# A decoder layer on one core: attention's steps draw products forward by a table, more rooms, other first loads, a later second norm

## The chip, the cores and the metric

The kernel runs on one core of a Trainium2 chip. The core has a matrix engine (PE, with its weight loads shown as PEld), a vector engine (DVE), a scalar engine (ACT), a general engine (POOL) and an engine that here issues transfers (SP). Each takes its instructions in order; they wait for one another through semaphores. The metric is the time of one execution on the device, in microseconds.

## The reference

One layer on x of 1024 tokens by 1024 features, all in float32:

```
h = rms_norm(x); proj = h @ w_in              # 256 pool columns, then q, k, v of 12 heads of 64
q, k = rope(q), rope(k)
pool_out = means over 2/4/8/16 tokens minus the token, per group @ w_pool, * pool_scale
attn_out = merge, by softmax denominators, of three windows: (128,1), (512,4), (2048,16)
x = x + rms_norm(concat(pool_out, attn_out) @ w_out)
h = rms_norm(x); f = (silu(h @ w_gate) * (h @ w_up)) @ w_down     # w_gate, w_up: 1024 x 2816
x = x + rms_norm(f)
```

## The kernel before

Products are float32 made of three passes: each operand is split into a high part (ACT, a rounding copy) and a low part (a subtraction on DVE or POOL), and high·high, high·low and low·high are summed in one bank. A pass is a matmul of 128 x 128 by 128, 256 or 512 columns. Features lie on partitions, tokens along the free dimension, in two halves of 512 (`h`).

The program has these stages.

1. **First loads.** x comes in eight tiles (`load_x`, L242 and L243 scale and split it), the first two weight tiles in two chunks (`load_w`, L155 and L159), and `first` makes q and k of head pair 0. The squares of x (L249, L251) feed the first norm.
2. **Attention.** Twelve *units*, each one pair of heads and one half. A unit runs `scores` (eight steps; DVE takes masked scores from a bank `ps_s` with a row minimum into `sx`, L556; ACT makes the exponentials in `pp`, L559), `merge` (small tiles `ex`, `em`, `dd`, `wv`; the two windows' sums are put together by two products `ps_s<-ex,ls`, L575 to L595), `weigh` (POOL, L611, or DVE, L609, multiply `pp` by `wv`) and `values`: `turn` transposes four blocks of `pp` into a bank `ps_t` (L119), ACT and DVE split it into `ptr` (L655, L656), and `product` multiplies `ptr` with v into `ps_o`; at the end of a head the low half is added (L691) and split into `mix` (L621, L623), which goes to memory (`mixd`, L628). v takes the way over memory: projected, split, written (`vd<-vs`, L475), read again in two orders (`v<-vd`, L504).
3. Beside it runs **fill**: the projections of the next pairs (ps_pj, and ropes of their results: `rsw`, `rco`, L323 to L328, DVE and POOL), v's projection and the pool mixer. They are lists of single products (`Fill`).
4. **Output projection** of both halves, then per half a `chain`: norm, sum with x, split for the next stage, squares of the new x (L1004, L1005) and its norm's factor (`s3.mean`, `s3.rows`).
5. **Gate, up and down**, in seven block products per block of columns (Strassen's scheme), and the last norm and sum.

What sets the order: a plan. Each list of steps has a start and an end in units (`PRM`), and `emit` sorts all steps by their time. PE's instructions stay in that written order; the others are placed by a scheduler that works from estimated times. Inside a step `await_` keeps a small model clock: where a result that the step needs is not due yet, it first draws fill products (`pull`), at most twelve:

```
    def await_(*keys):
        at = max([due.get(k, 0.0) for k in keys] or [0.0])
        n = 0
        while clock[0] < at and n < G["fl"]:
            ...
            pull()
            n += 1
```

Rooms: `pp` (also the tiles of x and other small loads) has 7 of 4 KB a partition, `ptr` 2, the raw weight tile `wraw` 2.

Of the kernel before, what the change touches and what calls it, by code (L numbers as in the profile page):

```python
# [15 lines left out]
P = 128  # L16
# [6 lines left out]
PPB = 7  # L23
PTB = 2
# [10 lines left out]
        'sqa': (1, 0, 0, 1, 0, 0, 0, 1),  # L35
        'we': (1, 1, 1, 0, 0, 0, 0, 0, 0, 0, 1, 1),
        'nt0': 0.505,
        'nt1': 0.51,
        'oq': (0, 1, 1, 1, 0, 0, 0, 1),
        'lag': 3.0,  # L40
        'fl': 12,
        'lt': 3.0,
        'ls': 2.2,
        'lm': 2.8,
        'lw': (3.5, 0.5),
        'nm': 0.02,
# [49 lines left out]
        'c0': (0.13, 0.2, 0.21, 0.6, 0.3, 0.7, 0.9, 0.99),
        'c1': (0.08, 0.17, 0.18, 0.8, 0.4, 0.95, 1.57, 1.7),
        'c2': ((0.95, 1.35), (1.4, 1.6)),
        'e0': ((0.26, 0), (0.42, 0), (0.47, 0.9)),
        'e1': (((1.08, 0), (1.28, 0), (1.3, 1.9)), ((2.0, 0), (2.01, 0), (2.02, 2.03)))}  # L100
# [10 lines left out]
def hybrid_block(ctx: ExitStack, tc: tile.TileContext, xT, w_in, w_v, w_pin, w_pool, w_out, w_gate, w_up, w_down,  # L111
# [6 lines left out]
    def turned_to(dst, src, by):  # L118
        return tc.keep_in_program_order(nc.tensor.transpose(dst, src, by))  # L119

# [33 lines left out]
    def split(dst, src, eng):  # L154
# [3 lines left out]
        for at in range(0, n, w):  # L158
            eng.tensor_tensor(dst[:, 1, at:at + w], src[:, at:at + w], dst[:, 0, at:at + w].bitcast(F32), ALU.subtract)  # L159
# [39 lines left out]
    nc.sync.dma_start(g1s, g1)  # L199
# [17 lines left out]
    w0r = [wpool.tile([P, 1024], F32, name="wraw", tag="wraw", bufs=2) for i in range(2)]  # L217
# [4 lines left out]

    def first(i, k):
        for a, b in PASSES:
            for h in range(2):
                mm(acc0[i, h], w0[i][:, a, k * P:(k + 1) * P], xk[k][:, b, h * 512:(h + 1) * 512],
                   start=(k == 0 and a + b == 0), stop=(k == NK - 1 and a == 1))

    def load_w(i, lo, hi):
# [3 lines left out]
        split(w0[i][:, :, sl], w0r[i][:, sl], nc.vector)  # L233

    xr0 = []

    def load_x(k, lo=0, hi=T):
        if lo == 0:
            xr0.append(att.tile([P, T], F32, name="xraw", tag="pp", bufs=PPB))
        r, sl = xr0[k], slice(lo, hi)  # L240
        nc.sync.dma_start(r[:, sl], xT[:, k, sl])
        nc.scalar.activation(xk[k][:, 0, sl], r[:, sl], AF.Copy, scale=g1s[:, k:k + 1])  # L242
        nc.vector.scalar_tensor_tensor(xk[k][:, 1, sl], r[:, sl], g1s[:, k:k + 1], xk[k][:, 0, sl].bitcast(F32),  # L243
                                       op0=ALU.mult, op1=ALU.subtract)

    def square(k):
        r = xr0[k]
        d = att.tile([P, T], F32, name="jk", tag="ptr", bufs=PTB) if k else sq
        nc.scalar.activation(d, r, AF.Square)  # L249
# [7 lines left out]
    for i in range(2):  # L257
        first(i, 0)
# [1308 lines left out]
```

## Time and profile before

| | us |
|---|---|
| median of 3 runs | 1169.71 |
| lowest and highest | 1167.99, 1169.85 |
| the profiled execution | 1170.79 |
| its span, first to last instruction | 1169.0 |

Busy time in that span: PE 1135.2 us (97%), weight loads 982.6 (84%), DVE 791.9 (68%), POOL 603.2 (52%), ACT 543.5 (46%). The mean granted clock of PE is 0.988 of its full speed. The span has three parts: first loads and attention up to some 465 us, the turn to the feed-forward part to some 512 us, and the feed-forward products to the end.

To read it: a row of a group gives line, engine, operation, what is written and read, and times in us; in rows of the order of time the bracket gives the idle time before an instruction and who ended it. A busy PE is one with some matmul in flight, not one at its peak. The line numbers are those of the kernel before.

### The profile page before, as it was taken

How to read it: one execution, taken by the hardware profiler on the slowest of the kernel's cores; microseconds unless marked ns; L12 is line 12 of the kernel's file. 1: busy time of each engine (PE TensorE's matmuls, PEld its weight loads, DVE VectorE, ACT ScalarE, POOL GpSimd, SP SyncE). 2: the span in 40 equal slices, each digit the busy share in tenths (PEclk: the TensorE clock that was granted, in tenths of full speed). 3: DMA queues.
4: the chain of work that ended last, by engine and by line, in shares of the span. 5: the costliest groups of instructions: out<-in, count | busy, mean ns of one | idle time of the engine just before them, and what ended most of it. 6: DMA issues, size and time to landing. Idle time of an engine off the chain costs nothing.

```text
span 1169.0 us, 17248 instructions
## 1 busy us (share of the span) xinstructions
PE 1135.2 (97%) x6134; PEld 982.6 (84%) x6134; DVE 791.9 (68%) x1477; ACT 543.5 (46%) x1033; POOL 603.2 (52%) x541
## 2 busy tenths in 40 slices
PE   8999999999998999999999999999999999999996
PEld 6998889989888888778888888888888888888896
DVE  7766778787887675869685665756565475454685
ACT  7356667665566674655432233223232335343430
POOL 0111546565565413150476667777665978656521
PEclk9999999999999999989999999999999999999998
DMA  7315151515124744732143544544535859766542
GB/s 270 102 60 181 37 181 37 168 49 181 55 73 146 286 163 163 272 106 90 52 174 135 198 162 175 186 173 161 206 128 188 281 198 378 240 204 191 183 144 72
DMA packets 85365, 188.51 MB, mean 161 GB/s; under 512 B 8736, under 2 KB 24352, under 8 KB 83872
## 3 DMA queue, kind: packets, MB, share of 16 engines
q1 hardware_dynamic: 84704, 186.90, 45.9%
q8 instruction: 48, 0.79, 0.3%
q10 hardware_dynamic: 576, 0.52, 0.1%
q14 instruction: 37, 0.30, 0.1%
HBM read 134.44 MB, written 52.95 MB: 160 GB/s over the span
## 4 chain that ended last, share of the span: by engine, by line
PE 83%; DVE 6%; ACT 4%; DMA 3%; issue 2%; POOL 1%; SPq 0%; ACTq 0%; POOLq 0%; DVEq 0%
PE ps_pj L116 28%; PE ps_o L116 22%; PE ps_s L116 21%; PE ps_t L116 9%; PE ps_t L119 2%; ACT pp L559 1%; DMA b<-in_w_out_dram 1%; DMA m<-mixd 1%; DMA mixd<-mix 1%; DVE k L348 1%; DMA xraw<-in_xT_dram 1%; DMA rw<-in_w_up_dram 0%; DVE ptr L656 0%; DVE whl L159 0%; DMA vd<-vs 0%
## 5 line engine op out<-in xcount | busy, mean ns | idle before, releaser
L116 PE MATMUL ps_pj<-x,whl 128*128 128x512 f32 x480 | 145.6, 417 | 0.0
L1221 POOL TENSOR_TENSOR fw<-rw,fw 128x512 fp32r<-128x512 f32 x74 | 101.6, 1399 | 61.3 <-ACT fw L1219 58.7
L611 POOL TENSOR_SCALAR pp<-pp,wv 128x256 f32<-128x256 f32 (+1 forms) x156 | 72.1, 482 | 103.8 <-DVE wv L595 51.0
L116 PE MATMUL ps_o<-tT,fw 128*128 128x512 f32 x504 | 117.5, 389 | 0.0
L159 POOL TENSOR_TENSOR whl<-wraw,whl 128x512 fp32r<-128x512 f32 x50 | 66.4, 1348 | 91.4 <-ACT whl L155 55.8
L116 PEld LDWEIGHTS ps_o<-tT,fw 128*128 128x128 f32 x504 | 94.6, 188 | 19.6
L559 ACT ACTIVATE pp<-pp,sx 128x128 f32<-128x128 f32 (+1 forms) x192 | 89.3, 468 | 30.1 <-DVE sx L556 29.6
L116 PEld LDWEIGHTS ps_pj<-x,whl 128*128 128x128 f32 x480 | 87.4, 194 | 10.2 <-POOL whl L159 0.4
L1221 POOL TENSOR_TENSOR whl<-rw,whl 128x512 fp32r<-128x512 f32 x42 | 61.1, 1479 | 58.3 <-ACT whl L1219 58.3
L1219 ACT ACTIVATE fw<-rw 128x1024 fp32r<-128x1024 f32 x37 | 38.5, 1057 | 97.5 <-DVE rw L1187 41.9
L116 PE MATMUL ps_pj<-whl,x 128*128 128x256 f32 x528 | 79.5, 291 | 0.0
L1363 POOL TENSOR_TENSOR op<-rw,op 128x512 fp32r<-128x512 f32 x38 | 59.9, 1577 | 37.3 <-ACT op L1362 36.0
L656 DVE TENSOR_TENSOR ptr<-ps_t,ptr 128x512 fp32r<-128x512 f32 (+1 forms) x84 | 56.2, 669 | 24.4 <-ACT ptr L655 23.8
L1362 ACT ACTIVATE op<-rw 128x1024 fp32r<-128x1024 f32 x38 | 40.2, 1060 | 66.9 <-PE ps_t L116 31.3
L325 POOL TENSOR_TENSOR rsw<-rsw,sinr 128x512 f32<-128x512 f32 x20 | 26.2, 1312 | 85.0 <-DVE rsw L323 85.0
L116 PEld LDWEIGHTS ps_pj<-whl,x 128*128 128x128 f32 x528 | 69.7, 194 | 0.4 <-DVE whl L159 0.2
L655 ACT ACTIVATE ptr<-ps_t 128x512 fp32r<-128x512 f32 (+1 forms) x84 | 48.4, 576 | 41.0 <-PE ps_t L119 39.7
L116 PE MATMUL ps_o<-ptr,v 128*128 128x128 f32 (+1 forms) x472 | 59.2, 259 | 5.4 <-DVE ptr L656 5.4
L116 PE MATMUL ps_pj<-b,fw 128*128 128x512 f32 x264 | 61.6, 389 | 0.0
L116 PEld LDWEIGHTS ps_o<-ptr,v 128*128 128x128 f32 x472 | 52.8, 165 | 9.8 <-DVE ptr L656 6.5
L116 PEld LDWEIGHTS ps_pj<-b,fw 128*128 128x128 f32 x264 | 49.5, 188 | 10.3
L116 PE MATMUL ps_s<-k,qh 128*128 128x128 f32 (+1 forms) x192 | 53.6, 291 | 0.3 <-DVE sx L556 0.2
(302 smaller groups left out, 2918.0 us busy)
## 6 DMA issues: line engine op xcount, KB each, us to landing
rw<-bd SPq DMA_DIRECT2D x77, 256.0 KB, 4.9
v<-vd SPq DMA_DIRECT2D x22, 512.0 KB, 4.4
rw<-wsd SPq DMA_DIRECT2D x44, 256.0 KB, 4.0
rw<-in_w_gate_dram SPq DMA_DIRECT2D x20, 512.0 KB, 3.6
rw<-in_w_up_dram SPq DMA_DIRECT2D x20, 512.0 KB, 4.6
bd<-p SPq DMA_DIRECT2D x33, 256.0 KB, 3.0
rw<-in_w_down_dram SPq DMA_DIRECT2D x33, 256.0 KB, 4.8
fw<-in_w_down_dram SPq DMA_DIRECT2D x16, 512.0 KB, 4.1
```

The costliest lines, as they stand in the source:

```text
L116: return tc.keep_in_program_order(nc.tensor.matmul(*a, **k))
L119: return tc.keep_in_program_order(nc.tensor.transpose(dst, src, by))
L159: eng.tensor_tensor(dst[:, 1, at:at + w], src[:, at:at + w], dst[:, 0, at:at + w].bitcast(F32), ALU.subtract)
L325: eng[0].tensor_tensor(s, s, sinr[:, sl], ALU.mult)
L559: nc.scalar.activation(pt[:, j, lo:], pt[:, j, lo:], AF.Exp, bias=sx[:, 0, side, j, hd, 0:1], scale=-1.0, accum_out=sx[:, 0, side, j, hd, ...
L611: nc.gpsimd.tensor_scalar(pv, pv, un.wv[:, side, j, hd:hd + 1], 1.0, op0=ALU.mult, op1=ALU.mult)
L655: nc.scalar.activation(ptr[:, 0, :w], t[:, :w], AF.Copy)
L656: nc.vector.tensor_tensor(ptr[:, 1, :w], t[:, :w], ptr[:, 0, :w].bitcast(F32), ALU.subtract)
L1219: nc.scalar.activation(w[n][:, :, 0], raw[n], AF.Copy)
L1221: low[0] = nc.gpsimd.tensor_tensor(w[n][:, i, 1], raw[n][:, i], w[n][:, i, 0].bitcast(F32), ALU.subtract)
L1362: nc.scalar.activation(w[:, :, 0], raw, AF.Copy)
L1363: nc.gpsimd.tensor_tensor(w[:, 0, 1], raw[:, 0], w[:, 0, 0].bitcast(F32), ALU.subtract)
```

## The change

It has five parts.

- The program's scratch memory for transfer descriptors is set to 1 KB, and three rooms are added: `pp` 8, `ptr` 3, `wraw` 3.
- A table `x` gives, by unit and step, a number of fill products that the step draws beside those of the model clock; a negative number lets the step begin earlier on that clock. Each unit has its own start and end times (`own`).
- The first loads come in another order, g1 on ACT's queue, x1 in two halves, the weights in chunks of two, two and four blocks; the first half tile of x gets its high part on DVE; the passes of x0 and x1 go by half.
- Half 0's second norm: its `mean` and `rows`, and the scaling of z by g3, leave the list of the output projection (`cut`) and stand 0.25, 0.42 and 0.25 to 0.7 into the list of the first gate and up products. Their results are held in their banks until the rows are there (`kept`). The weights of the second column block are loaded by steps of that list.
- More of DVE's instructions keep the written order (`pinned`), the pool mixer's products go by four tiles, and several times of the plan differ.

Three places, engine by engine. First DVE at the merge of unit 7 (pair 3, half 1), where `ex` is each window's sums, `rsw` and `rco` the rope of a projection and `ps_o`, `low` the end of a head. Before:

```order
L575 TENSOR_TENSOR ex<-sx,qdB 128x64
L691 TENSOR_TENSOR ps_o<-ps_o,low 64x512
L656 TENSOR_TENSOR ptr<-ps_t,ptr 128x512
L323 STREAM_SHUFFLE rsw<-ps_pj 128x512
L324 TENSOR_TENSOR rco<-ps_pj,cosr 128x512
L575 TENSOR_TENSOR ex<-sx,qdA 128x64
```

and after:

```order
L776 TENSOR_TENSOR ptr<-ps_t,ptr 128x512
L811 TENSOR_TENSOR ps_o<-ps_o,low 64x512
L694 TENSOR_TENSOR ex<-sx,qdA 128x64
L448 STREAM_SHUFFLE rsw<-ps_pj 128x512
L449 TENSOR_TENSOR rco<-ps_pj,cosr 128x512
```

The rope now stands behind the second `ex`. In unit 1 the rope stays before it and the addition into `ps_o` moves behind; in unit 5 both stand before it:

```order
L448 STREAM_SHUFFLE rsw<-ps_pj 128x512
L449 TENSOR_TENSOR rco<-ps_pj,cosr 128x512
L811 TENSOR_TENSOR ps_o<-ps_o,low 64x512
L694 TENSOR_TENSOR ex<-sx,qdA 128x64
```

Second, PE at the end of the output projection of half 1 (`fw` is the mix, `b` the normed x of half 0, `ps_t` the first gate bank, `ones,sq` the sums of squares, `idt,nrr` a norm's rows). Before:

```order
L116 MATMUL ps_pj<-fw,whl 128x512 x24
L116 MATMUL ps_s<-fw,whl 128x512 x5
L116 MATMUL ps_o<-ones,sq 128x1 x4
L116 MATMUL ps_s<-fw,whl 128x512 x18
L119 MATMUL ps_o<-idt,nrr 128x128 x4
L116 MATMUL ps_s<-fw,whl 128x512
```

and after, where the same place has neither, and the first sums to come, 12 gate products later, are those of half 1's first norm:

```order
L193 MATMUL ps_pj<-fw,whl 128x512 x24
L193 MATMUL ps_s<-fw,whl 128x512 x24
L193 MATMUL ps_t<-b_5468,whl 128x512
L193 MATMUL ps_t<-b_5469,whl 128x512
L193 MATMUL ps_t<-b_5468,whl 128x512 x2
```

Third, SP's first transfers. Before:

```order
L199 DMA g1s<-in_g_dram 128x8
L241 DMA xraw<-in_xT_dram 128x512
L232 DMA wraw<-in_w_in_dram 128x256
L241 DMA xraw<-in_xT_dram 128x512
L232 DMA wraw<-in_w_in_dram 128x256
L241 DMA xraw<-in_xT_dram 128x1024
L232 DMA wraw<-in_w_in_dram 128x768 x2
L241 DMA xraw<-in_xT_dram 128x1024 x6
```

and after:

```order
L324 DMA wraw<-in_w_in_dram 128x256
L338 DMA xraw<-in_xT_dram 128x512
L324 DMA wraw<-in_w_in_dram 128x256
L338 DMA xraw<-in_xT_dram 128x512 x3
L324 DMA wraw<-in_w_in_dram 128x256 x2
L338 DMA xraw<-in_xT_dram 128x1024
L324 DMA wraw<-in_w_in_dram 128x512 x2
L338 DMA xraw<-in_xT_dram 128x1024 x5
```

x2 now stands behind 256 KB of weights where 768 KB stood, and x1 before them in two pieces.

The core of the diff:

```diff
-PPB = 7
-PTB = 2
+PPB = 8
+PTB = 3
...
+ 'own': {0: {'s0': 0.4799, 's1': 0.5663, 'm': 0.8618, 'w0': 1.0668, 'w1': 0.9699, 't0': 1.1072, 'v0': 1.259, 'v1': 1.9554},
...
+PRM["x"] = {(0, 'm'): 5, (0, 's', 0): 8, (0, 's', 1): 6, (0, 's', 2): 5, (0, 's', 3): 3, (0, 's', 4): 2, (0, 's', 6): 3,
...
-        r = own or wpool.tile([P, 1024], F32, name="wraw", tag="wraw", bufs=2)
+        r = own or wpool.tile([P, 1024], F32, name="wraw", tag="wraw", bufs=3)
...
-    nc.sync.dma_start(g1s, g1)
+    nc.scalar.dma_start(g1s, g1)
...
+    def split_x(k, lo=0, hi=T, fast=False):
+        r, sl = xr0[k], slice(lo, hi)
+        if fast:
+            pinned(nc.vector.tensor_scalar(xk[k][:, 0, sl], r[:, sl], g1s[:, k:k + 1], None, op0=ALU.mult))
+        else:
+            pinned(nc.scalar.activation(xk[k][:, 0, sl], r[:, sl], AF.Copy, scale=g1s[:, k:k + 1]))
...
+    fetch_w(0, 2, 0)
+    fetch_x(0, 0, 512)
+    fetch_w(0, 2, 1)
+    fetch_x(0, 512, T)
+    for h in range(2):
+        fetch_x(1, h * 512, h * 512 + 512)
     for i in range(2):
+        fetch_w(2, 4, i)
+    fetch_x(2)
     for i in range(2):
+        fetch_w(4, NK, i)
+    for k in range(3, PPB):
+        fetch_x(k)
...
+    for k in range(2):
+        for h in range(2):
+            for i, n in ((0, 0), (1, 0), (0, 2), (1, 2), (0, 1), (1, 1)):
+                part(i, h, k, n)
...
-    def await_(*keys):
+    def await_(*keys, step=None):
 
         at = max([due.get(k, 0.0) for k in keys] or [0.0])
-        n = 0
-        while clock[0] < at and n < G["fl"]:
+        more, n = G["x"].get(step, 0), 0
+        while clock[0] < at + min(0, more) * 0.235 and n < G["fl"]:
             f = Fill.now
             if f is None or f.n >= len(f.steps):
                 break
             pull()
             n += 1
+        for n in range(more):
+            pull()
...
-            await_(("s", 0))
+            await_(("s", 0), step=(unit_of[pr.p, h], "s", 4 * hd + 2 * (1 - side) + jj))
...
-        await_(("m", pr.p, h))
+        await_(("m", pr.p, h), step=(unit_of[pr.p, h], "m"))
...
         return [([load], -1, 0), ([sq.mean], at[0], 0), ([sq.rows], at[1], 0),
                 ([lambda d=d: add(d) for d in range(NK)], at[2], at[3]),
-                ([lambda d=d: whole(d) for d in range(NK)], at[4], at[5]),
-                ([s3.mean], at[6], 0), ([lambda: s3.rows(r3[:, sl])], at[7], 0)]
+                ([lambda d=d: square(d) for d in range(NK)], at[4], at[5]),
+                ([s3.mean], at[6], 0), ([rows], at[7], 0),
+                ([lambda d=d: scale(d) for d in range(4 if h else NK)], at[8], at[9])]
...
-    emit((st, 0.0, 1.0), *chain(0, *sqs[0], G["c0"]))
+    first_half = chain(0, *sqs[0], G["c0"])
+    emit((st, 0.0, 1.0), *first_half[:G["cut"]])
...
-    before = [x for f in range(EARLY) for x in gate_up(f, 0, ws[f])] + one[0] + one[1]
+    before = [x for f in range(EARLY) for x in gate_up(f, 0, ws[f], kept)] + one[0] + one[1]
...
     emit((before, 0.0, 1.0), (beside, 1.0, 1.0 + ratio), (one[2], 1.0 + ratio, 1.0 + ratio + len(one[2]) / len(before)),
-         *chain(1, *sqs[1], G["c1"]),
-         ([ahead], 0.1, 0), ([let_go], G["c1"][7] + 0.001, 0),
+         *first_half[G["cut"]:], ([lambda: let_go(kept)], G["c0"][7] + 0.001, 0), *chain(1, *sqs[1], G["c1"]),
+         *(([lambda a=(f, i): next_weights(*a)], G["ew"][i], 0) for f in range(1, EARLY) for i in range(2)),
+         ([ahead], 0.1, 0), ([lambda: let_go(held)], G["c1"][7] + 0.001, 0),
...
-    nc = _bacc.Bacc("TRN2", target_bir_lowering=False, num_devices=1)
+    nc = _bacc.Bacc("TRN2", target_bir_lowering=False, num_devices=1, dynamic_dma_scratch_size=1024)
```

More of the change, by code (lines that the diff above doesn't have):

```diff
@@ L119, in turned_to, with pinned, did, need @@
         return tc.keep_in_program_order(nc.tensor.transpose(dst, src, by))
+    def pinned(x):
+        return tc.keep_in_program_order(x)
+    seen = {}
+    def did(key):
+        seen[key] = seen.get(key, 0) + 1
+    def need(key, n):
+        assert seen.get(key, 0) >= n, (key, n, seen.get(key, 0))
     const = ctx.enter_context(tc.tile_pool(name="const", bufs=1))
@@ L216, in hybrid_block @@
     w0 = [wpool.tile([P, 2, 1024], F32R, name="whl", tag="whl", bufs=2) for i in range(2)]
-    w0r = [wpool.tile([P, 1024], F32, name="wraw", tag="wraw", bufs=2) for i in range(2)]
+    w0r = [wpool.tile([P, 1024], F32, name="wraw", tag="wraw", bufs=3) for i in range(2)]
     acc0 = {}
@@ L273, in hybrid_block @@
     nc.sync.dma_start(sinr, sint)
-    for k in (NK - 2, NK - 1):
+    for k in range(NK - 3, NK):
         square(k)
-    wv0 = wtile(w_v[0][0], nc.vector, qkp, "k")
     mA = cload(maskA, [P, 256], "mA", qkp)
@@ L282, in hybrid_block @@
     pmt = cload(perm, [P, P], "pmt", con1)
-    for k in (NK - 2, NK - 1):
-        for i in range(2):
+    for i in (1, 0):
+        for k in (NK - 2, NK - 1):
             first(i, k)
@@ L305, in norm_rows @@
         nc.scalar.activation(rb[:, sl], pb, AF.Copy)
-    def pinned(x):
-        return tc.keep_in_program_order(x)
+        did(("rb", h))
     def tables(h):
         sl = slice(h * 512, (h + 1) * 512)
+        need(("turns", h), 1)
+        need(("rb", h), 1)
+        did(("tables", h))
         for x in (cosr, sinr):
@@ L666, in product @@
             need(("t", pr.p), 2 if h == 0 else 4)
-            await_(("ptr", pr.p, h, hd, gi), ("v", pr.p, h))
+            await_(("ptr", pr.p, h, hd, gi), ("v", pr.p, h), step=(unit_of[pr.p, h], "v", hd * len(groups) + gi))
             clock[0] += 0.7
@@ L722, in pool_proj @@
                 pool.u[h] = [att.tile([P, 4, 256], F32R, name="u%d" % b, tag="v%d%d" % (b, h), bufs=1) for b in range(2)]
-            us = [(pool.ps[:, x % 2 * 256:x % 2 * 256 + 256], norm["r"][:, x:x + 1], *(pool.u[h][b][:, x % 4] for b in range(2)))
+            us = [(pool.ps[tt // 2][:, x % 2 * 256:x % 2 * 256 + 256], norm["r"][:, x:x + 1], *(pool.u[h][b][:, x % 4] for b in range(2)))
                   for x in (tt - 1, tt)]
@@ L729, in pool_proj @@
             due["u", h] = clock[0] + 3.2
+            did(("u", h))
     def pool_bands():
@@ L839, in hybrid_block @@
         g = dict(G, **G["h1" if h else "h0"])
-        g.update(**(G["first"] if u == 0 else {}), **(G["last"] if u == 11 else {}))
+        g.update(G["own"].get(u, {}))
         st = later(scores, pr, h)
@@ L1092, in half_of @@
     def half_of(h):
+        need(("r3", h), 1)
         return r3[:, h * 512:(h + 1) * 512]
@@ L1101, in products @@
                 box[i] = bank("s" if i else "t")
+            need(("x1", h, k), 1)
             for a, b in PASSES:
@@ L1132, in block_sum @@
         (h, d), b, to = SUMS[n][:3]
+        for hh, dd in ((h, d), b if isinstance(b, tuple) else (h, d)):
+            need(("x1", hh, dd + c), 1)
+            need(("s3", hh, dd + c), 1)
+            need(("g3", hh, dd + c), (hh, dd) != (1, 4))
         a, b = z[h](d + c), S[b][c] if isinstance(b, str) else z[b[0]](b[1] + c)
@@ L1282, in run, with let_go @@
             emit((steps, 0, 1))
-    held = [lambda: None]
-    def let_go():
+    held, kept = ([lambda: None] for n in range(2))
+    def let_go(held):
         while held:
@@ L1293, in hybrid_block, with next_weights @@
         ahead = ahead()
-    ws += [{0: ftile(w_gate[f], f), 1: ftile(w_up[f], f)} for f in range(1, EARLY)]
-    before = [x for f in range(EARLY) for x in gate_up(f, 0, ws[f])] + one[0] + one[1]
+    ws += [{} for f in range(1, EARLY)]
+    def next_weights(f, i):
+        with tc.issue_after(powers[-1].ins):
+            ws[f][i] = ftile((w_gate, w_up)[i][f], f)
+    before = [x for f in range(EARLY) for x in gate_up(f, 0, ws[f], kept)] + one[0] + one[1]
     beside = [x for f in range(EARLY) for x in gate_up(f, 1, ws[f], held)]
```

207 lines of the change are left out of this document (90 added, 117 removed), and 130 rows, old and new, of the table PRM.

## The prediction

> **What bounds the kernel now.** I read the head of the page first, then busy time by stage, then what the matrix engine (PE) waited for, and last the clock around those waits.
>
> ```profile
> span 1169.0 us, 17248 instructions
> PE 1135.2 (97%) x6134; PEld 982.6 (84%) x6134; DVE 791.9 (68%) x1477; ACT 543.5 (46%) x1033; POOL 603.2 (52%) x541
> ```
>
> PE is busy 1135.2 of 1169.0 us; no other engine is over 68%. The change adds and removes no product, so it can only win back the 33.8 us of idle time and what follows from it. The stages, from the busy time in stretches (length, then PE, weight load, DVE, ACT, POOL, granted clock, DMA):
>
> ```profile
> 119.00:157.00 38.00, 34.48 (x242) 31.84 (x240) 30.40 (x87) 22.67 (x59) 20.61 (x24) 0.96 0.18 57
> 303.00:400.00 97.00, 88.66 (x563) 80.60 (x562) 79.11 (x225) 61.62 (x165) 52.60 (x65) 0.95 0.42 148
> 465.00:512.00 47.00, 43.64 (x188) 35.74 (x188) 35.24 (x43) 29.58 (x50) 14.71 (x10) 0.93 0.66 245
> 512.00:1140.00 628.00, 627.85 (x2858) 522.90 (x2857) 394.27 (x462) 226.78 (x276) 395.92 (x277) 1.00 0.51 180
> ```
>
> From 512 us on there is nothing to win: 0.15 us of idle time in 628, at some 0.22 us a product (627.85 over 2858), and what follows is code that the change leaves alone. Three stretches of attention and of the turn to the feed-forward part hold 3.5, 8.3 and 3.4 us of idle time, at a clock of 0.93 to 0.96. What PE waited for (total, times, longest):
>
> ```profile
> PE ps_o L116 <- DVE ptr L656: 5.4, 5, 1.5
> PE ps_s L116 <- DVE ex L575: 4.5, 3, 2.5
> PE ps_t L119 <- POOL pp L611: 3.0, 2, 2.7
> PE ps_o L116 <- DVE sq L1005: 2.7, 1, 2.7
> PE ps_s L116 <- DVE x L243: 1.6, 2, 1.0
> PE ps_o L116 <- DVE mix L625: 0.9, 1, 0.9
> PE ps_pj L116 <- DMA m<-mixd: 0.9, 1, 0.9
> PE ps_s L116 <- ACT x L242: 0.7, 2, 0.5
> ```
>
> These make 19.7 us, and the change touches the place of each. The clock, in stretches cut where it changes (the granted clock is the third figure from the end):
>
> ```profile
> 119.32:122.73 3.41, 1.91 (x17) 1.69 (x16) 3.41 (x7) 1.21 (x4) 2.17 (x2) 1.00 0.00 0
> 122.73:126.15 3.42, 3.42 (x12) 2.69 (x11) 3.24 (x10) 1.98 (x4) 0.38 (x1) 0.54 0.00 0
> ...
> 204.66:208.07 3.41, 1.96 (x18) 1.76 (x17) 3.38 (x8) 2.17 (x9) 2.68 (x2) 1.00 0.30 82
> ...
> 303.64:307.05 3.41, 0.89 (x10) 0.75 (x8) 3.41 (x7) 2.70 (x7) 1.51 (x2) 1.00 0.00 0
> ...
> 341.19:344.60 3.41, 1.86 (x11) 1.24 (x10) 3.31 (x7) 1.64 (x4) 2.31 (x3) 1.00 0.34 120
> ...
> 371.90:375.32 3.42, 0.88 (x8) 0.67 (x6) 3.35 (x5) 0.00 (x0) 3.42 (x4) 1.00 0.61 179
> ...
> 501.62:505.03 3.41, 1.00 (x5) 0.50 (x3) 2.69 (x5) 3.27 (x6) 0.00 (x0) 1.00 0.47 154
> 505.03:511.85 6.82, 6.49 (x19) 5.51 (x20) 3.19 (x3) 2.22 (x6) 4.37 (x3) 0.52 0.27 79
> ```
>
> Each stretch of 3.41 us in which PE was busy 1.91 us or less is followed by one at half clock; the one with 1.96 is not. Half clock for 3.41 us costs about 1.7 us of work, for 6.82 us about 3.4. Five drops, 4 × 1.7 + 3.4 = 10.2 us: a stall of 1.6 us or more is paid twice.
>
> [...]
>
> **The change, part by part.** Gains are negative.
>
> The smaller descriptor scratch frees the memory for the rooms. The transfers in the rows of this text are all issued by SP, none by POOL, so I price it at 0; a transfer that did need it would be among the slower cases.
>
> First loads. PE waited 1.6 + 0.7 us for x. Weights now come first, x1 in two halves, the next two weight chunks before x2, and the first x is scaled on DVE while ACT takes the weights. 1.8 of the 2.3 us and a little of the start: −2.0. Ends: −2.8 (all, and 0.5 us of the start), and +1.0, one more of the longest wait of that kind, should x3, which now has 512 KB of weights straight ahead of it, come late instead of x2.
>
> The merges. In unit 7 the second product waits 2.52 us for ex:
>
> ```profile
> 303.14 0.22 DVE L575 TENSOR_TENSOR ex<-sx,qdB 128x64 f32<-128x64 f32 x1
> ...
> 304.59 0.72 DVE L323 STREAM_SHUFFLE rsw<-ps_pj 128x512 f32<-128x512 f32 x1
> ...
> 305.21 0.68 DVE L324 TENSOR_TENSOR rco<-ps_pj,cosr 128x512 f32<-128x512 f32 x1
> ...
> 305.80 1.01 DVE L575 TENSOR_TENSOR ex<-sx,qdA 128x64 f32<-128x64 f32 x1
> ...
> 306.86 0.43 PE L116 MATMUL ps_s<-ex,ls 128*128 128x64 f32 x2 [2.52 <-DVE ex L575]
> ```
>
> The rope's shuffle and cosine stand before ex, and ex itself takes 1.01 instead of 0.22 us beside POOL's part of the rope. The new order has ex before both: 0.72 + 0.68 + 0.79 = 2.2 us earlier, and PE has two more products (0.4 us) ahead. The wait goes. In unit 1:
>
> ```profile
> 119.00 0.69 DVE L691 TENSOR_TENSOR ps_o<-ps_o,low 64x512 f32<-64x512 f32 x1 [0.81 <-ACT low L690]
> ...
> 120.84 0.98 DVE L575 TENSOR_TENSOR ex<-sx,qdA 128x64 f32<-128x64 f32 x1
> ...
> 121.88 0.43 PE L116 MATMUL ps_s<-ex,ls 128*128 128x64 f32 x2 [1.50 <-DVE ex L575]
> ```
>
> the rope stays before ex, but the 0.69 us sum goes behind it: 0.7 to 0.8 us of the 1.50 stay. The third wait (0.5 us, unit 9) gets 0.6 us more PE work and goes. Together 4.5 − 0.8 = −3.7. What is late next: the rope behind ex, by 0.2 us, and it feeds a later unit. Against it, unit 5 loses: its order now has the rope and that sum before ex, and only 3.0 us of PE work between its last score and the merge where 4.3 stood; by unit 1's delay (1.50 beyond 3.6 us of work, less the 0.7) that is a new wait of 4.4 − 3.0 = +1.4. Ends for all merges: −4.5 and +1.0 (nothing won in unit 1, unit 5 twice as bad, one more).
>
> The turned weights (ptr). Five waits, 5.4 us. With a third room and the table, the PE work between a group's turn and its product grows in the order: over the 84 groups the lower quartile goes from 3.3 to 4.2 us. At the five places it goes from 3.4 to 3.7, 3.2 to 2.7, 3.4 to 4.9, 3.2 to 4.4 and 2.8 to 3.0. The second keeps its wait, since DVE still holds ptr behind a long split:
>
> ```profile
> 149.12 1.40 DVE L355 TENSOR_TENSOR ql<-rco,qh 64x512 fp32r<-64x512 f32 x2
> ...
> 151.29 0.79 PE L116 MATMUL ps_o<-ptr,v 128*64 128x128 f32 x7 [1.52 <-DVE ptr L656]
> ```
>
> and the fifth most of its own. I count 2.6 us gone; against that four other groups fall to 2.2 to 2.7 us, below any of before (2.8, no wait): +1.0. Sum −1.6; ends −5.4 and +2.
>
> The weighed scores.
>
> ```profile
> 372.60 2.49 POOL L159 TENSOR_TENSOR whl<-wraw,whl 128x512 fp32r<-128x512 f32 x2
> ...
> 375.49 0.87 PE L119 MATMUL ps_t<-idt,pp 128*128 128x128 f32 x3 [2.71 <-POOL pp L611]
> ```
>
> POOL splits a weight for 2.49 us ahead of the weighing; its order keeps that. PE has 0.9 us more to do (four products): −0.9; ends −3.0 and 0.
>
> Half 0's second norm.
>
> ```profile
> 505.36 1.84 PE L116 MATMUL ps_o<-ones,sq 128*128 128x1 f32 x8 [2.74 <-DVE sq L1005]
> ...
> 505.56 2.96 POOL L159 TENSOR_TENSOR whl<-wraw,whl 128x512 fp32r<-128x512 f32 x2 [5.52 <-ACT whl L155]
> ```
>
> PE stands 2.74 us, from 502.6 on, before the sums of squares. They now come 12 steps of 3 products, some 8 us, into gate and up, whose results are held until the rows are there. The wait goes, and the next thing late is the first gate weight: PE is there after the 19 products that stood behind the wait, at 502.6 + 19 × 0.22, about 507, and POOL has the first half of the low parts in 505.56 + 1.48, 507.0 too. I leave +0.6 for it: −2.1; ends −2.7 and 0. The scalings of z, listed later, still stand among ACT's rows ahead of that weight, so they free nothing.
>
> The mixer output's wait (0.9) and the loads of the mix (0.9; the projection starts later, its last load slightly earlier): −1.3; ends −1.8 and 0.
>
> The clock. The drops behind unit 1, unit 7 and the norm lose their cause: 1.7 + 1.7 + 3.4 = −6.8. Those at 345 and 375 us stay, as their stalls mostly do. Ends: −10.2, and 0.
>
> Sum: −2.0 − 3.7 + 1.4 − 1.6 − 0.9 − 2.1 − 1.3 − 6.8 = −17.0 us. The profiled execution took 1170.8 us (span 1169.0, 1.8 around it), 1.1 above the median of 1169.7: 1170.8 − 17.0 − 1.1 = 1152.7, so **1153 us**. All good ends together make −30.4 us, 1139; all bad ones +4.0, 1174.
>
> **The rivals.**
>
> *More goes than I count.* Of my sum there stay 0.8 + 1.4 us at merges, 2.8 + 1.0 at ptr, 2.1 at POOL, 0.6 at the gate weight and 3.4 of clock: 12.1 us. For it: a wait that shrinks also lets the next engine start sooner. Three quarters of that: 1144.
>
> [...]
>
> *The waits move.* A unit's supply of products is fixed; drawn forward, it leaves later steps bare. DVE is busy 30.4 of 38 us in the first of the three stretches. If the attention waits come back elsewhere, start, norm and its clock remain, 2.0 + 2.1 + 3.4 = 7.5: 1162.
>
> *Slower: SP's queue blocks the values.* SP now issues three weight loads, among them one for room not yet free, ahead of the third write of the values to memory, where one stood before; the reload stands behind that write.
>
> ```profile
> 69.25 0.37 SPq L475 DMA_DIRECT2D vd<-vs  x1
> ...
> 104.55 2.31 SPq L504 DMA_DIRECT2D v<-vd  x4
> ...
> v<-vd SPq DMA_DIRECT2D x22, 512.0 KB, 4.4
> ...
> vd<-vs SPq DMA_DIRECT2D x12, 512.0 KB, 4.1
> ```
>
> If the write is held until PE stands before the first product of a unit, the stall is a write and a reload, 8.5 us, and 1.7 of clock. From two such (20 us against my 17) it is slower; with three, 1153 + 31 = 1184. Against it: 35 us lie between the last of these writes and the first reload, which stands behind writes of the mixer and not behind this one.
>
> **How the numbers follow.** Forecast 0.54, more 0.20, clock 0.08, moved 0.11, slower 0.07. A difference of 0.2% (2.3 us) is what can be told from none. The range 1142 to 1164 reaches over both middle rivals and most of the lower one; outside lie the slower one, some of the lower, and the tails. Faster: all but the slower rival and the bad end of the moved waits, 0.89; same 0.04; slower 0.07. If only the cases that are faster are kept, 1142 to 1162.
>
> **What would show it.** Right: no wait for ex in unit 7, under 1 us in unit 1; no wait for sq before the gate; granted clock 1.00 where 0.93 to 0.96 stood, save one or two stretches; x waits of 0.5 us. [...]

## The result and the profile after

The changed kernel takes 1155.72 us (median of 4 runs, 1155.04 to 1157.07), the kernel before 1169.78 beside it: a ratio of 0.9884, 95% interval 0.9867 to 0.9902, or 13.6 us less by that ratio (14.1 between the medians). The profiled execution took 1155.71 us. Head of its page:

```profile
span 1153.9 us, 17223 instructions
PE 1128.3 (98%) x6134; PEld 979.2 (85%) x6134; DVE 790.1 (68%) x1481; ACT 545.4 (47%) x1035; POOL 604.1 (52%) x541
```

The span is 15.1 us shorter. PE's idle time went from 33.8 to 25.6 us (-8.2), its busy time from 1135.2 to 1128.3 (-6.9) with the same 6134 products: the second part is mostly clock (5.1 of the 6.9, priced below). What PE waited for now (total, times, longest; two rows that did not change, 1.5 us before the first product and 0.9 in the last norm, are left out):

```profile
PE ps_t L196 <- POOL pp L730: 3.1, 3, 1.8
PE ps_pj L196 <- POOL nrr L273: 3.0, 2, 2.0
PE ps_pj L193 <- DVE whl L248: 2.9, 1, 2.9
PE ps_o L193 <- DVE sq L1130: 1.5, 1, 1.5
PE ps_o L193 <- DVE ptr L776: 1.2, 2, 0.8
PE ps_s L193 <- DVE ex L694: 0.8, 1, 0.8
PE ps_o L193 <- ACT ptr L775: 0.6, 1, 0.6
PE ps_s L193 <- DVE x L346: 0.6, 1, 0.6
PE ps_o L193 <- DVE mix L744: 0.2, 1, 0.2
```

The rows of ex, ptr, x and mix have shrunk. The row of sq is another wait than before: now it is half 1's first norm. Two things have grown: a wait for the low parts of a weight (whl, 2.9 us), and that for the rows of half 1's second norm, which is 2.0 of the 3.0 us of nrr and stands at 557 us. The other 1.0 us belongs to the layer's last norm, at 1144 us, and was there before. Before, nrr had these two lines, of which 0.15 us were half 1's second norm:

```profile
PE ps_pj L119 <- POOL nrr L184: 1.2, 2, 1.0
PE ps_o L119 <- POOL nrr L184: 0.6, 1, 0.6
```

The clock drops three times where it dropped five times. Stretches of the changed kernel around them, two to a drop (granted clock third from the end). As in the prediction, the cuts lie 0.24 us ahead of the recorded changes, so half clock reads 0.53 or 0.54:

```profile
300.11:303.52 3.41, 1.44 (x7) 0.72 (x6) 3.18 (x11) 1.47 (x4) 0.67 (x2) 1.00 0.17 71
303.52:306.94 3.42, 3.40 (x11) 2.68 (x12) 3.35 (x8) 1.19 (x2) 3.42 (x8) 0.54 0.00 0
358.15:361.56 3.41, 1.57 (x15) 1.36 (x13) 3.31 (x6) 1.56 (x2) 3.41 (x5) 1.00 0.61 192
361.56:364.98 3.42, 3.42 (x17) 3.40 (x18) 2.70 (x6) 2.33 (x4) 3.42 (x7) 0.53 1.00 326
477.60:481.02 3.42, 1.13 (x5) 0.59 (x4) 3.42 (x6) 1.11 (x3) 0.00 (x0) 1.00 0.00 0
481.02:484.43 3.41, 2.76 (x7) 2.18 (x8) 3.41 (x5) 3.41 (x7) 0.00 (x0) 0.53 0.43 139
```

The three drops lie on a fixed grid: the 177.50 us from 303.52 to 481.02 us are 52 steps of 3.413 us, and the drop at 361.56 us lies 17 of them behind the first. The third is at the new wait for whl. In order of time, around it:

```profile
469.47 7.93 POOL L1367 TENSOR_TENSOR op<-rw,op 128x512 fp32r<-128x512 f32 x4 [17.65 <-DMA x1d<-z]
471.05 8.23 DVE L1165 SCALAR_TENSOR_TENSOR b<-z,g3s,b 128x512 fp32r<-128x512 f32 x6
480.41 1.21 DVE L248 TENSOR_TENSOR whl<-wraw,whl 128x1024 fp32r<-128x1024 f32 x1
481.67 6.66 PE L193 MATMUL ps_pj<-fw,whl 128*128 128x512 f32 x22 [2.94 <-DVE whl L248]
```

DVE needs 8.23 us for six instructions that make b, while POOL splits the first weights of the block products (`rw`) beside it: 1.78 us each for the four beside POOL, 0.74 for the two behind it. The weight that PE waits for stands behind them. Before, these six took 4.07 us and POOL split `rw` after them:

```profile
487.80 4.07 DVE L1040 SCALAR_TENSOR_TENSOR b<-z,g3s,b 128x512 fp32r<-128x512 f32 x6
493.99 6.05 POOL L1221 TENSOR_TENSOR op<-rw,op 128x512 fp32r<-128x512 f32 x4 [22.48 <-ACT op L1219]
```

So the first gate product came 20.7 us earlier than before (493.6 against 514.3 us), but the last product only 15.2. The experiments ask three things: what each part is worth, why the turn to the feed-forward part gave back some of it, and what the clock does. Each ratio below is to the kernel before on the same chip.

### The profile page after: what moved, and what is told of

The parts are those of the page before. It is cut to its first block, busy times and chain, and to the rows that moved or that the text cites. A ratio compares the mean times of both kernels' runs of the same rounds, so it can differ in the third digit from the quotient of the medians.

```text
span 1153.9 us, 17223 instructions
## 1 busy us (share of the span) xinstructions
PE 1128.3 (98%) x6134; PEld 979.2 (85%) x6134; DVE 790.1 (68%) x1481; ACT 545.4 (47%) x1035; POOL 604.1 (52%) x541
## 4 chain that ended last, share of the span: by engine, by line
PE 80%; DVE 9%; issue 3%; DMA 3%; ACT 2%; POOL 1%; SPq 0%; POOLq 0%; DVEq 0%; ACTq 0%
PE ps_pj L193 28%; PE ps_o L193 22%; PE ps_s L193 20%; PE ps_t L193 7%; PE ps_t L196 3%; DMA wraw<-in_w_out_dram 1%; DVE sq L1130 1%; ACT pp L678 1%; DVE z L1162 1%; DMA b<-in_w_out_dram 1%; DVE z L1163 1%; DVE pp L675 1%; DVE tT L1291 1%; DMA xraw<-in_xT_dram 1%; DMA wraw<-in_w_gate_dram 1%
## 5 line engine op out<-in xcount | busy, mean ns | idle before, releaser
L193 PE MATMUL ps_pj<-x,whl 128*128 128x512 f32 x480 | 143.1, 410 | 0.0
L193 PE MATMUL ps_o<-ptr,v 128*128 128x128 f32 (+1 forms) x472 | 56.4, 254 | 1.8 <-DVE ptr L776 1.2
```

Source lines behind the costliest of these rows:

```text
L193: return tc.keep_in_program_order(nc.tensor.matmul(*a, **k))
```

## The experiments

**The clock, and DVE beside POOL, by themselves.** This kernel leaves the whole layer out, and was executed once. PE runs bursts, and a chain of DVE instructions of growing length stands between them; then DVE works alone and beside POOL:

```diff
+ for n in range(0, 12):
+     ps = burst(50 + (7 * r + 3 * n) % 15, gap(ps, n, 128))
...
+ for m in range(12):
+     nc.vector.scalar_tensor_tensor(b, a, s, x, op0=ALU.mult, op1=ALU.subtract)
+ for m in range(6):
+     nc.gpsimd.tensor_tensor(c, a, x, ALU.subtract)
```

> This kernel leaves the whole layer out: its output is tiles of x. It measures two disputed prices by themselves. First, PE runs bursts of 50 to 64 products of 512 columns, and before each burst waits for a chain of 2 to 13 small instructions of DVE, so that 60 idle times of about 1.3 to 3.5 us fall at many places in time. Second, DVE does 8 instructions of the kind that makes b (512 columns, two operands and a scalar column) alone, and then 12 of them beside six subtractions of 512 columns on POOL. My reading of the clock (a stretch of 3.41 us with PE busy 1.91 us or less is followed by one at half clock, 1.96 is not): idle times under 1.4 us bring no drop, those of 1.5 to 3.0 us bring one in some cases, by where they lie against a fixed grid of 3.41 us, and none under about 1.5 us in any stretch does. [...] For DVE beside POOL: the changed kernel's rows have 0.68 us for one such instruction alone and 1.37 beside POOL's subtraction. If the two hold each other up, the 12 take 1.2 to 1.4 us each while POOL runs; if the cause there was another one, they take 0.7 throughout.

Of the 60 idle times, five of each length, none of 1.24, 1.51 or 1.77 us brought half clock; of those of 2.03, 2.29, 2.55 and 2.81 us 10 in 20 did; all 25 of 3.08 us and more did. So 20 of the 45 that are shorter than 3.41 us, the time between changes of the clock, brought it. Stretches of that length, the second right behind the first:

```profile
469.47:472.88 3.41, 1.38 (x6) 0.84 (x6) 1.80 (x5) 0.00 (x0) 0.00 (x0) 1.00 0.00 0
472.88:476.29 3.41, 3.41 (x11) 2.60 (x10) 0.00 (x0) 0.00 (x0) 0.00 (x0) 0.53 0.00 0
264.67:268.08 3.41, 1.74 (x8) 1.12 (x6) 1.50 (x5) 0.00 (x0) 0.00 (x0) 1.00 0.00 0
```

The first and the third hold an idle time of the same 2.03 us: wholly inside one stretch it brings a drop (PE busy 1.38), cut by a stretch's end it does not (1.74). My expected 1.5 us of idle time was too low. Cut at the recorded changes, the stretches of this run that lie at full clock part cleanly: the 35 with PE busy 1.46 us or less are each followed by half clock, the 213 with 1.50 us or more are not. In the layer, whose products are of mixed sizes, that is no bound: 1.91 us brought half clock before the change, and 2.46 us did in the run with the norm's move alone, below. What exactly is counted stays open. The other price, one instruction of DVE alone and then the six of DVE and of POOL that ran side by side:

```profile
L225 DVE SCALAR_TENSOR_TENSOR da<-x,ds 128x512 f32<-128x512 f32 x8 | 6.0, 752 | 15.1 <-ACT da L221 14.9
1047.14 9.97 DVE L231 SCALAR_TENSOR_TENSOR db<-da,ds,x 128x512 f32<-128x512 f32 x6
1046.59 9.97 POOL L233 TENSOR_TENSOR dc<-da,x 128x512 f32<-128x512 f32 x6 [1046.15 <-DVE dc L229]
```

Alone an instruction of DVE took 0.75 us. Of the twelve, the first was over before POOL began (0.75), the next six took 1.63 each beside POOL's six (1.60 each), and the last five 0.75 again. The two hold each other up: they take turns, one of each in 1.67 us, and each of DVE's six ended some 0.55 us behind the one of POOL that ran when it began. The 1.63 us are more than twice the time alone. What makes them take turns no run shows.

**The rw loads later.**

```diff
-    with tc.issue_after(behind.ins):
+    with tc.issue_after(loads[-1].ins):
         ahead = ahead()
```

> The changed kernel, with one thing moved: the raw weights of the feed-forward block products (rw) are issued after the loads of the second half of the first up weight, not behind the loads of the output projection. The changed kernel has a new wait of 2.94 us of PE before the out projection's product at 481.67 us, for the low parts of a weight on DVE, and a half-clock stretch beside it (1.7 us). My theory: the third raw-weight room lets SP reach the rw loads 35 us earlier (449.1 instead of 484.6 us), POOL splits them at 469 to 477 us, beside DVE's six instructions that make b, which then take 1.37 us each instead of 0.68, and the weight split queued behind them comes 3 us late. Then this kernel wins 2.9 + 1.7: about 1151. The rival: DVE is behind at this place because the moved norm puts its work together otherwise; then the wait stays, and the time is 1155.7 within 1 us.

1155.13 us, ratio 0.9877 (0.9859 to 0.9894): no gain that can be told. Yet the mechanism is as said. Rows of this run:

```profile
468.93 4.06 DVE L1165 SCALAR_TENSOR_TENSOR b<-z,g3s,b 128x512 fp32r<-128x512 f32 x6
483.23 7.95 POOL L1367 TENSOR_TENSOR op<-rw,op 128x512 fp32r<-128x512 f32 x4 [32.83 <-ACT op L1365]
491.14 7.29 POOL L248 TENSOR_TENSOR whl<-wraw,whl 128x512 fp32r<-128x512 f32 x4
492.90 2.50 PE L193 MATMUL ps_t<-b,whl 128*128 128x512 f32 x5 [4.88 <-POOL whl L248]
```

b takes 4.06 us again, the wait for whl on DVE is gone, and the first two gate products stand at 487.4 us, 6.2 earlier. But POOL now splits rw ahead of the gate weight's low part, and PE waits 4.88 us for that, with 6.83 us at half clock behind it. The gain was real and was paid back at once.

**wraw back at two rooms.**

```diff
-name="wraw", tag="wraw", bufs=3)
+name="wraw", tag="wraw", bufs=2)
```

> The changed kernel, with the raw weight tile wraw back at two rooms, the other two new rooms (pp 8, ptr 3) kept. My theory: with two rooms SP reaches the rw loads late again, POOL does not run beside DVE's b instructions, and the wait of 2.9 us and its half clock (1.7 us) go: about 1151, if nothing of attention hung on this room. If the third room did save something in attention or at the first loads, that is lost: 1152 to 1156. The rival (DVE's backlog from the moved norm): the wait stays, 1155.7 or, without the room, more.

1154.73 us, ratio 0.9867 (0.9851 to 0.9883). The wait of 2.9 us for whl is gone; in its place PE waits 0.4 us for the gate weight, 1.6 before the sums of half 1's first norm, 1.8 for the second up weight and 1.4 for the rows of half 1's second norm. The third raw room is worth nothing in the changed kernel.

**The same, with half 1's norms later.**

```diff
- 'c1': (0.08, 0.17, 0.18, 0.8, 0.4, 0.95, 1.57, 1.7, 0.6, 0.94),
+ 'c1': (0.12, 0.21, 0.22, 0.8, 0.4, 0.95, 1.57, 1.77, 0.6, 0.94),
```

> The kernel with wraw at two rooms (1154.73), and half 1's norms a little later in their list: the first norm's mean at 0.12 of the list instead of 0.08, its rows at 0.21 instead of 0.17, the rows of the second at 1.77 instead of 1.70. In the trace with two rooms PE waits 1.56 us for the sums of squares of the first norm and 1.4 us for the rows of the second. My theory: these are only late by their place, the products drawn ahead cover them, and nothing waits behind them: 1154.7 - 1.6 - 1.4 = 1151.7. The rival: DVE and POOL are behind by more than the products cover and each wait comes back at the next thing that they make (z's sums, gate's weight): 1154.7 within 1 us.

1154.57 us, ratio 0.9879 (0.9862 to 0.9895): the rival. The wait for the sums shrank to 0.2 us and that for the rows went, but that for the second up weight grew from 1.8 us:

```profile
PE ps_s L193 <- POOL fw L248: 3.5, 1, 3.5
...
507.50 4.89 DVE L1163 TENSOR_TENSOR z<-z,xr 128x512 f32<-128x512 f32 x8
507.69 5.83 POOL L248 TENSOR_TENSOR fw<-wraw,fw 128x512 fp32r<-128x512 f32 x1 [3.23 <-ACT fw L244]
```

With the norms later, POOL's first subtraction for that weight begins beside the first of eight additions of DVE. It took 5.83 us and ended 1.1 us behind the last of them; with the earlier norms the same subtraction met only the end of that run and took 2.42.

**The rw loads between, all rooms kept.**

```diff
+    with tc.issue_after(loads[-1].ins):
+        ahead = ahead()
     ws = [{0: ftile(w_gate[0], 0), 1: ftile(w_up[0], 0)}]
```

with the later norms of the run above.

> The changed kernel, all three rooms kept, with two things moved: the raw weights of the block products (rw) are issued after the last load of the output projection and ahead of the first gate weight (behind it, PE waited 4.9 us for that weight, since POOL split rw first; at the place of the changed kernel it waited 2.9 us for DVE), and half 1's norms a little later in their list, as in the run with wraw at two rooms. In the two-room runs 5.8 us of waits were left at the turn (0.6 gate weight, 1.8 sums of squares, 1.9 the next gate weight, 1.5 the rows), and moving the norms alone brought nothing, as the wait for the next gate weight grew from 1.9 to 3.6 us: with two rooms its load goes out at 503 us. My theory: with the third room that load is early, POOL splits rw after DVE's b instructions, and 4 to 5 us go: 1150 where the kernel before takes 1169.7 (a ratio of 0.983). The rival: POOL and DVE have no more to give here, each wait that goes comes back at the next weight: 1154 to 1156 (0.987).

1155.11 us, ratio 0.9879 (0.9863 to 0.9896): the rival again. There is no trace of it that can be compared, so where the waits came back was not seen. Four orders of the turn end within 0.9867 to 0.9879, none to be told from the change's 0.9884.

**Half 0's second norm back.**

```diff
- 'c0': (0.13, 0.2, 0.21, 0.6, 0.3, 0.7, 0.25, 0.42, 0.25, 0.7),
- 'cut': 5,
+ 'c0': (0.13, 0.2, 0.21, 0.6, 0.3, 0.7, 0.9, 0.99, 0.3, 0.7),
+ 'cut': 8,
```

> The changed kernel, with half 0's second norm (its mean and rows, and the scaling of z) back in the list of the output projection, as before the change; everything else as changed. The prediction had 2.1 us of wait and 3.4 us of clock won by the move: this kernel should then be 5.5 us slower, 1161. My theory after the traces: the first gate product came 20.7 us earlier than before the change, but the last matmul only 15.2, so what the move won was given back by waits for half 1's norms (1.62 and 2.15 us) and for the out projection's weight (3.1 us with half clock): the move is worth 0 to 2 us, and this kernel takes 1156 to 1158.

1170.49 us, ratio 1.0007 (0.9996 to 1.0018): all of the gain is gone, 14 us, more than either expectation. Attention is as fast as in the changed kernel (its last product at 441.2 us, there 443.1). Three places carry the loss. PE waits 4.2 us before the sums of that norm, and runs 6.83 us at half clock. Some 30 us later it waits 1.3 and 1.9 us for the second up weight, with 3.41 us at half clock. And 76 us after the sums POOL has the rows of half 1's second norm behind three groups of weight splits, and another 6.83 us at half clock follow:

```profile
PE ps_o L193 <- DVE sq L1130: 4.2, 1, 4.2
...
557.85 2.52 POOL L1367 TENSOR_TENSOR whl<-rw,whl 128x512 fp32r<-128x512 f32 x2 [2.92 <-ACT whl L1365]
560.33 2.53 POOL L1367 TENSOR_TENSOR fw<-wraw,fw 128x512 fp32r<-128x512 f32 x2
562.82 4.93 POOL L1367 TENSOR_TENSOR fw<-rw,fw 128x512 fp32r<-128x512 f32 x4
567.70 1.01 POOL L273 TENSOR_TENSOR nrr<-nrr,half 128x4 f32<-128x4 f32 x1
568.76 1.12 PE L196 MATMUL ps_pj<-idt,nrr 128*128 128x128 f32 x4 [5.42 <-POOL nrr L273]
```

In the changed kernel the same row stands ahead of the two fw groups. Its time in the list was not touched: the scheduler, which places POOL's instructions by estimated times, put it elsewhere.

**The same with wraw at two rooms**, to see whether the early rw loads make the difference: both edits above together.

> The changed kernel with half 0's second norm back in the list of the output projection and wraw at two rooms. With the norm back alone the time was that of before the change (1170.5), though the move alone in the kernel before won 3.5 us. My theory: the early rw loads (third raw room) make DVE and POOL late just there (b instructions of 1.37 us, POOL's splits ahead of the norm's rows: waits of 4.2 us for the sums and 5.4 for the rows of half 1), and the norm's move hides this; with two rooms the norm's place is worth 4 to 6 us: 1159 to 1161 where before takes 1169.7 (0.991 to 0.993). The rival: in the changed order the norm's place is worth some 15 us whatever the room: 1168 to 1171 (0.999 to 1.001).

1169.08 us, ratio 1.0004 (0.9992 to 1.0015): the rival. The waits are nearly the same, 3.6 us for the sums and 5.4 for the rows, so it is not the early loads.

**The norm's move alone**, in the kernel before:

```diff
-    emit((st, 0.0, 1.0), *chain(0, *sqs[0], G["c0"]))
+    first_half = chain(0, *sqs[0], G["c0"])
+    emit((st, 0.0, 1.0), *first_half[:5])
...
+         *first_half[5:], ([lambda: let_go(kept)], G["c0"][7] + 0.001, 0), *chain(1, *sqs[1], G["c1"]),
```

> The kernel before, with the norm's move alone: half 0's second norm (sums, rows, the scaling of z) goes from the list of the output projection into that of the first gate and up products, at the places that the change gives them, with their results held until the rows are there. Attention, rooms, loads and weights stay as before. The prediction had 2.1 us of wait and 3.4 of clock: 1164.2. After the run that took the move back out of the changed kernel (1170.5 against 1155.7) my theory is that its worth depends on what DVE and POOL have to do there: here, without the early loads of rw, the wait of 2.74 us and the half clock of 3.4 go, and at most 1 us comes back for the gate weight: 1164 to 1165. Two rivals: the move is worth all of 14.8 us by itself (1155), or its waits come back at the next weight and norm (1168 to 1170).

1164.92 us, ratio 0.9970 (0.9959 to 0.9981), 3.5 us less where the kernel before took 1168.0: my theory's mechanism, at two thirds of its size. The 2.74 us and the 6.82 us of half clock are gone, the first gate product comes 9.1 us earlier, and then half 1's first sums are late (the second and later rows; the first is explained below):

```profile
101.07:104.48 3.41, 2.46 (x22) 2.37 (x21) 1.51 (x4) 2.19 (x7) 0.00 (x0) 1.00 0.21 86
...
507.25:510.66 3.41, 1.97 (x13) 1.53 (x12) 2.00 (x2) 0.26 (x3) 2.94 (x2) 1.00 0.51 156
510.66:514.07 3.41, 3.41 (x10) 2.65 (x9) 0.00 (x0) 1.05 (x2) 3.26 (x3) 0.54 0.54 154
...
509.50 1.02 PE L116 MATMUL ps_o<-ones,sq 128*128 128x1 f32 x8 [1.44 <-DVE sq L1005]
```

1.44 us and one stretch of 3.41 at half clock (1.7) of the 5.5 come back.

Up to 500 us PE, DVE, ACT and POOL have the same instructions in the same order as in the kernel before, and yet half clock fell otherwise. Before, it began at 123, 307, 345 and 376 us; here at 105, behind the first row, and at 306 and 374. The wait of 1.50 us in unit 1 was paid twice there and not here. So in these two executions the place of the grid decided in part which stalls cost a stretch at half clock.

**The changed kernel without the table.**

```diff
+PRM["x"] = {}
- 'vt': (..., (8.9599, 10.177), (9.83, 10.1116)),
+ 'vt': (..., (8.9599, 10.27), (9.83, 10.29)),
```

> The changed kernel with its table x emptied: no step draws more, or fewer, fill products than the model clock asks for. (The last two of the times of v's loads are set so that v is there for the products that now come earlier; rooms, the units' own times, first loads and the norm stay as changed.) My theory: the table carries attention's gain, which the traces put at 3.7 us at the merges, 3.6 at the turned weights, 1.6 at the mix and some of the clock. Without it 8 to 12 us are lost: 1164 to 1168, with waits for ex and ptr of 8 us or more. The rival: the rooms and the units' own times do it, and the table is decoration: within 3 us of 1155.7.

1166.58 us, ratio 0.9978 (0.9967 to 0.9990), against the change's 0.9884, as my theory had it: in this order the table is worth some 11 us. With rooms, loads and the norm's move but without the draws, PE waits again:

```profile
PE ps_t L197 <- POOL pp L731: 6.1, 3, 3.3
PE ps_o L194 <- DVE ptr L777: 3.4, 3, 1.7
PE ps_s L194 <- DVE ex L695: 2.3, 2, 1.9
```

The last product of attention stands at 454.9 us (443.1 with the table, 458.3 before). That 8 us of ex and ptr would be waited for was too much (5.7); pp makes up for it.

**The rooms alone**, in the kernel before: pp 8, ptr 3, wraw 3 and the smaller descriptor scratch.

```diff
-PPB = 7
-PTB = 2
+PPB = 8
+PTB = 3
```

> The kernel before with the three rooms and the smaller descriptor scratch alone: no table, the old times, loads and norm. My theory: rooms alone save little, as the order of PE does not draw on them, 0 to -3 us; at the turn the third raw room lets the rw loads go out early and costs some of it: -3 to +5 against before (0.997 to 1.004). The rival: the rooms give most of what the change wins, 8 us or more (0.993 or less).

1183.80 us, ratio 1.0124 (1.0107 to 1.0141): 14.5 us slower, outside both expectations. PE's instructions stand in the same order as before; the scheduler has placed DVE's, ACT's and POOL's otherwise. An example, in unit 10:

```profile
383.48 3.20 DVE L355 TENSOR_TENSOR ql<-rco,qh 64x512 fp32r<-64x512 f32 x2
388.00 2.13 DVE L159 TENSOR_TENSOR xk<-wraw,xk 128x1024 fp32r<-128x1024 f32 x1
...
388.14 0.39 PE L116 MATMUL ps_s<-k,qh 128*128 128x256 f32 x1 [2.04 <-DVE sx L556]
390.97 0.57 PE L116 MATMUL ps_s<-k,qh 128*128 128x256 f32 x1 [1.46 <-DVE sx L556]
```

The low parts of q and a whole weight split, possible at that place since a room is free, stand between masked scores that PE's next products need; in the trace of before, that split comes behind these scores, at 394.64 us. Half clock follows (6.8 us), and at the turn two waits for sums, 5.2 us in all where before had 2.7.

**The first loads alone**, in the kernel before.

```diff
-    nc.sync.dma_start(g1s, g1)
+    nc.scalar.dma_start(g1s, g1)
...
+    fetch_w(0, 2, 0)
+    fetch_x(0, 0, 512)
+    fetch_w(0, 2, 1)
```

As in the changed kernel, the edit also pins the splits and the sums of squares, and puts v's first weight ahead of the last squares.

> The kernel before, with the new first loads alone (order of the transfers, g1 on ACT's queue, the first half tile of x on DVE, the passes of x0 and x1 by half). The traces have the end of the first products at 31.3 us before and 28.7 after, 2.7 earlier. The prediction's term is 2.0. My theory: the lead is kept, since what follows is bound by PE: 1167 (1166.5 to 1168). The rival: the lead is given back in the first units, which wait for other things (v, weights), so the time is that of before, 1169.7.

1179.57 us, ratio 1.0103 (1.0086 to 1.0120): 12 us slower. The x waits shrank (2.3 to 1.7 us), but the last sum of squares stands on DVE behind the ropes of four banks:

```profile
36.43 1.20 DVE L268 TENSOR_TENSOR sq<-sq,jk 128x1024 f32<-128x1024 f32 x1
...
37.69 2.50 PE L116 MATMUL ps_o<-ones,sq 128*128 128x1 f32 x11 [5.69 <-DVE sq L268]
```

**The same, with these ropes in written order.**

```diff
-        nc.vector.stream_shuffle(s, ps, SWAP16)
+        pin(nc.vector.stream_shuffle(s, ps, SWAP16))
...
-turn_by(acc0[i, h], h, sw[:, 0], c, eng("r%d" % (2 * h + i)), c)
+turn_by(acc0[i, h], h, sw[:, 0], c, eng("r%d" % (2 * h + i)), c, pinned)
```

> The kernel before with the new first loads, as in the run that lost 12 us, and one thing more that the change has: the ropes of the first q and k keep the written order on DVE, behind the sums of the squares of x. With the loads alone the scheduler put the ropes of four banks (5 us) ahead of the last of these sums; it ended at 37.6 us, PE stood 5.69 us before the first norm's product and then ran 10.2 us at half clock (5.1 us of work). My theory: this is all of the loss. Here all eight sums are done by some 33.4 us, PE, which is there at 32.0, waits 1.5 to 2 us, and the half clock goes or is one stretch of 3.4 us: 7 to 9 us less than with the loads alone, which is the time of before within 3 us (ratio 0.998 to 1.002 to before, where the loads alone had 1.010). The rival: the loss comes from the loads themselves or from what the scheduler does with all of DVE behind them (PE waited 3.5 us for masked scores in the first unit): 1.007 to 1.011.

1179.95 us, ratio 1.0082 (1.0068 to 1.0096). The time is in the rival's range. At its place the edit did part of what I said: the wait fell from 5.69 to 2.50 us (I had 1.5 to 2), the half clock from 10.2 to 6.8 (I had 3.4 or none), and attention's last product came at 463.9 us, not 470.1 (458.3 before). The rest went 490 us later, where nothing was edited:

```profile
525.36 3.48 POOL L162 TENSOR_TENSOR fw<-wraw,fw 128x512 fp32r<-128x512 f32 x2 [1.64 <-ACT nrr L182]
528.80 1.99 POOL L187 TENSOR_TENSOR nrr<-nrr,half 128x4 f32<-128x4 f32 x1
530.85 1.11 PE L119 MATMUL ps_o<-idt,nrr 128*128 128x128 f32 x4 [4.78 <-POOL nrr L187]
```

Without the pins these two rows of POOL stand the other way round. PE waits 4.78 us and a stretch of 6.83 us at half clock follows. So an edit at the program's start put one instruction of POOL behind another 490 us later.

## Why the prediction was right, and where it was not

Forecast 1153, measured 1155.7: the sum of -17.0 against -15.1 in the profiled spans. Its terms against the trace:

| step | predicted | trace |
|---|---|---|
| first loads (x) | -2.0 | -1.7 |
| merges (ex), with unit 5's new wait | -3.7 + 1.4 | -3.7 |
| turned weights (ptr) | -1.6 | -3.6 |
| weighed scores (pp) | -0.9 | +0.1 |
| half 0's second norm | -2.1 | +2.9 |
| mix and its loads | -1.3 | -1.6 |
| clock | -6.8 | -5.1 |

Together -12.7; the other 2.4 us are smaller waits (0.6) and PE's busy time beside half clock (1.8). The terms miss by up to 5.0 us, in both directions; that their sum came within 2 us is in part luck.

*First loads and merges.* As reasoned; the merge of unit 7 has no wait for ex, unit 1 none either. Unit 5's new wait (1.4) didn't come; the one left is 0.8 us in unit 10.

*Turned weights.* Mis-sized: the waits that I let stay or come (2.8 + 1.0) came to 1.8 in all.

*Weighed scores.* At the place that I priced it came as said: POOL still splits a weight ahead of the weighing, and the wait fell from 2.7 to 1.8 us. Two new waits of 0.7 and 0.6 us, at 123 and 303 us, took the gain.

*Half 0's second norm* is the step that failed. "The next thing late is the first gate weight" named one candidate out of four. The gate weight was on time. Late were the weight split for the output projection itself (2.94 us), half 1's first sums (1.5) and the rows of its second norm (2.0, where 0.15 stood). I had not followed what the third raw room, which has no term in my sum, lets SP and POOL do at this very place: rw is asked for at 449 us, where before it was 485, and its split falls beside DVE's work. With the wait moved elsewhere (the runs with rw later, or two rooms) another took its place each time, so this much idle time seems to belong to DVE and POOL at the turn; that is argued from four orders, not shown for all.

*The clock.* The reading held in the main: half clock without a long stall, in both traces behind the emptiest stretches, and the bursts confirm it apart from the layer. As a bound, 1.91 us did not hold: 1.97 and 2.46 us brought half clock in the run with the norm's move alone. (Cut at the recorded changes, PE's busy time in the prediction's five stretches is 1.91, 0.89, 1.69, 0.69 and 0.77 us; the reading is the same.) Three drops are left: that behind POOL's wait of unit 9, which I had kept; a new one behind three short waits at 300 us, while the one at 345, which I had kept too, went with its wait; and one at the new wait. The granted clock is 1.00 in the first of the three stretches of the prediction and 0.96 in the other two. In the run with rw later and in that with the norm back, attention has the same order and the same three waits at 300 us, and no drop there: a count of drops from one trace, mine of five and this one of three, is in part luck. The case "clock" with its chance of 0.08, that the drops stay though the waits go (1160), is not what the runs show: with the norm's move alone, the wait of 2.74 us and the 6.82 us of half clock behind it went together. The slower rival, SP's queue ahead of the values, did not show: the waits of PE have no row for v.

*That terms add up* is what the runs refute. Alone, the rooms cost 14.5 us and the loads 12, the norm's move wins 3.5; without the table the whole wins only 2.6 (ratio 0.9978), and with the norm back nothing (1.0007). I read the order of the changed program as it stands and priced that, which is why the sum came near; but no term is the worth of its edit. Rooms and pins had no term of their own. What a room does is to let the scheduler take work earlier, and at the places traced here what it took stood in front of what PE waits for.

## What to carry to other kernels

Where one engine's order is written and the others' are placed by a scheduler, price the built order as a whole, and never an edit by its own place: compare the rows of every engine, far from the edit too. Ahead of each wait that you remove, look for the work that a freed room or an earlier load lets run beside it, DVE beside POOL above all: an instruction of 0.75 us took 1.63 there. Count a stall of over two us nearly twice: 10 of the 20 idle times of 2.03 to 2.81 us and all 25 from 3.08 us on brought a stretch at half clock, 1.7 us of work.

## What was not expected of the hardware

- An instruction of DVE with two operands of 512 columns took 0.75 us alone and 1.63 beside POOL's subtractions, which took 1.60 each; the two took turns. A subtraction of POOL that began beside eight additions of DVE in a row took 5.83 us.
- Half clock came behind 20 of 45 idle times shorter than 3.41 us, from 2.03 us on. Of two of 2.03 us, the one wholly inside a stretch of the 3.41 us grid brought it, the one cut by a stretch's end did not. By my estimate each such stretch costs 1.7 us of work (3.41 us at a granted clock of 0.50), or twice that where it lasts 6.83.
